# Where the tensor engine's operands start in SBUF: tiles moved to multiples of 512 bytes

## The chip, the cores and the metric

The kernel runs on one core of one Trainium2 chip, as one launch. A core has a tensor engine (TensorE, PE in the profile; its weight loads are shown apart as PEld), a vector engine (VectorE, DVE), a scalar engine (ScalarE, ACT), GpSimd (POOL) and a sync engine (SyncE, SP), which here issues all the DMAs. The on-chip memory SBUF has 128 partitions; a tile takes the same bytes in each of them, and an address below is an offset within a partition. Matmul results go to another memory, PSUM. The metric is the device time of one execution in microseconds (us).

## The reference, cut to what matters

One layer of a decoder block on 256 tokens of width 2048, all float32:

```python
mod = (silu(c) @ w_mod + b_mod).reshape(B, 6, D)          # 2048 x 12288
sh1, sc1, g1, sh2, sc2, g2 = [mod[:, i, None, :] for i in range(6)]
h = rmsnorm(x, norm_mix) * (1.0 + sc1) + sh1
proj = h @ w_in                                           # 2048 x 5660, split into 14 parts
y = concatenate([gla(...), gated_deltanet(...), pool(...), forgetting_attention(...)])
x = x + g1 * (y @ w_out)                                  # 2048 x 2048
h = rmsnorm(x, norm_ffn) * (1.0 + sc2) + sh2
gate = causal_dwconv(h @ w_gate, conv_w) + conv_b         # 2048 x 5632
x = x + g2 * ((silu(gate) * (h @ w_up)) @ w_down)         # 2048 x 5632, 5632 x 2048
return rmsnorm(x, norm_final)
```

All six parts of `mod` come from one product of `silu(c)`, a row of 2048 numbers, with `w_mod`.

## The kernel before, in words

**Large products.** All five large products with x (`w_in`, `w_out`, `w_gate`, `w_up`, `w_down`) go through the tensor engine in the dtype float32r (f32r), one pass each, and are split in two terms: an operand is rounded to f32r (the high part) and the rest is rounded again (the low part); of the four products three are taken, high by high, high by low and low by high. The helper `split` (lines 114 to 116) does this: ScalarE copies with rounding (L115), VectorE subtracts (L116, the operation at L100). `load_split` loads a weight tile of 128 partitions by 1024 numbers into `wr` (five buffers) and splits it into `wh` and `wl` (three buffers each). The activations stand split in `bigA` (tile names `HL`, `Y2`, `H2`: for each of the 16 blocks of 128 features, 256 high and 256 low numbers) and, for the down projection, in `AH` and `AL`. All matmuls are issued by the helper `mm` (L97). The stationary operand (`lhsT`) is always 128 by 128 or narrower; the moving one has 256 or 512 columns.

**Stages.** First x, the rows of `c`, biases and norms are loaded and transposed (lines 285 to 330). Then the input projection: in four groups of four feature blocks, `mods` builds the modulated activations from `w_mod` on VectorE, `gdn` accumulates the gated DeltaNet's 12 feature blocks into the six PSUM tiles `acc`, and `pair` the other columns into `ext`. The four mixers follow, with the remaining columns of the input projection put between their steps, and with the products of `c` for the other parts of `mod` (`gemv`) running beside them on the tensor engine and VectorE. Then the output projection (`project`, PSUM tiles `ext` and `wot`), the second norm, gate and up projections (`proj`, PSUM tiles `fpt`), in 11 chunks of 512 columns, and the down projection, in column chunks of 512, 512, 512, 256 and 256, with the last two `gemv` beside it.

In `proj` the moving operand is `bigA`: for a feature block, 4 matmuls with `wh` as stationary operand and 512 columns (high and low at once), and 4 with `wl` and 256 columns. In the output and down projections the moving operand is `wh` or `wl`, 512 or 256 columns wide, and the stationary one `bigA` or `AH`/`AL`.

The mixers' own matmuls (PSUM tiles `gdt`, `oxt`) and the transposes are plain float32, on other tiles.

**Order of the work.** The program is written in the order of the code with some pieces interleaved by generators; a framework places the waits. DMAs are all issued by SyncE in program order.

**Where tiles lie.** A pool places its tiles one behind the other, in the order in which their tags first appear, each at a multiple of 32 bytes; a later pool begins behind the earlier ones that are open. The pool `keep` (L90) is the first: `ident`, `crow`, `ones`, `sel`, `V1`, `V2`, `V3`, `CB`, `cond`, `mhalf`, `s2`, `sh2`, then `bigA` (32768 bytes a partition), `bigC` (16384), `ga` (4096) and `x1s`. Behind it comes `wp` with `wr`, `wh`, `wl` and `wm`, 4096 bytes each, and behind that the pools of the phases: `cp` and, inside it, `sp` for the first phase, later `ap` with `AH` and `AL`, 45056 bytes each. `crow` (16 partitions by 128 numbers, 512 bytes) holds the rows of `c` until one transpose reads them (L309). `sh2` holds 16 numbers a partition, the second norm's shift; `x1s` holds the sums of squares of the chunks of the output projection, 2 by 5 numbers, and is read once by a reduction (L1000).

Of the kernel before, what the change touches and what calls it, by code (L numbers as in the profile page):

```python
# [8 lines left out]
F32 = mybir.dt.float32  # L9
# [7 lines left out]
P = 128  # L17
D = 2048
KT = D // P
T = 256  # L20
NT = T // P
# [52 lines left out]
def trunk_kernel(ctx: ExitStack, tc: tile.TileContext, x, c, w_mod, b_mod, norm_mix, norm_ffn, w_in,  # L74
# [3 lines left out]
    nc = tc.nc  # L78
# [11 lines left out]
    keep = ctx.enter_context(tc.tile_pool(name="keep", bufs=1))  # L90
    wp = ctx.enter_context(tc.tile_pool(name="wp", bufs=3))

    def kt_(shape, name, dt=F32):
        return keep.tile(shape, dt, name=name, tag=name)
# [26 lines left out]

    ident = kt_([P, P], "ident")
    nc.sync.dma_start(ident, cst[:, K_ID:K_ID + P])
    crow = kt_([KT, P], "crow")
    nc.sync.dma_start(crow, c[0].rearrange("(k p) -> k p", p=P))
    ones = kt_([P, P], "ones")
    V.memset(ones, 1.0)

# [10 lines left out]
    mhalf = kt_([P, 16], "mhalf")  # L139
    V.memset(mhalf, -0.5)  # L140
    s2 = kt_([P, KT], "s2")
    sh2 = kt_([P, KT], "sh2")

    bigA = lambda: keep.tile([P, KT, 2 * T], F32R, name="bigA", tag="bigA")
    bigC = lambda: keep.tile([P, KT * T], F32, name="bigC", tag="bigC")
# [82 lines left out]
    with ExitStack() as ph:  # L228
# [59 lines left out]
        with ExitStack() as st:  # L288
            sp = st.enter_context(tc.tile_pool(name="sp", bufs=1, reuse_waits="tile"))
            acp = st.enter_context(tc.tile_pool(name="acp", bufs=1, space=PSUM, reuse_waits="tile"))  # L290
            xt = sp.tile([P, NT, D], F32, name="xt")
            r1 = sp.tile([P, P], F32, name="r1")
            r2 = sp.tile([54, P], F32, name="r2")
            r3 = sp.tile([2 * NF, P], F32, name="r3")
# [652 lines left out]
        chunks = ((0, 512), (512, 512), (1024, 512), (1536, 256), (1792, 256))  # L947
# [26 lines left out]
        x1 = bigC().rearrange("p (t d) -> p t d", t=NT)  # L974
        for t in range(NT):
            nc.sync.dma_start(x1[:, t], x_v[:, t])
        x1s = kt_([P, NT, len(chunks)], "x1s")
        with tc.tile_pool(name="op", bufs=2, reuse_waits="tile") as op:
            for n, (c0, w) in enumerate(chunks):
                ns, gs = slice(c0, c0 + w), slice(c0 % 1024, c0 % 1024 + w)  # L980
# [11 lines left out]
    with ExitStack() as ph:  # L992
# [69 lines left out]
        with tc.tile_pool(name="op2", bufs=1, reuse_waits="tile") as op:  # L1062
            chunks = ((0, 512), (512, 512), (1024, 512), (1536, 256), (1792, 256))
            fs = op.tile([P, NT, len(chunks)], F32, name="fs")
            f1 = op.tile([P, 4], F32, name="f1")
            for n, (c0, w) in enumerate(chunks):
# [5 lines left out]
                for g in range(NF // nk):  # L1072
                    wh, wl = load_split(wd_v, nk * g, nk, c0, w)
                    for kk in range(nk):
                        k = nk * g + kk
# [55 lines left out]
```

## Time and profile before

| | |
|---|---|
| median of three runs | 1299.27 us (1299.02 to 1306.44) |
| profiled execution, its own time | 1303.01 us |
| span of its trace | 1301.2 us |
| mean granted TensorE clock | 0.985 |
| TensorE busy | 1248.5 us, 96% of the span |
| VectorE busy | 891.0 us, 68% |
| ScalarE busy | 636.7 us, 49% |
| read from HBM | 308.51 MB, 239 GB/s over the span |

The numbers of the trace are those of one execution. Busy times of matmuls overlap, since each is counted from its start to the end of its results; the distance from one start to the next is what a stream of them costs. In a group or a timeline row stand the line, the engine, the operation, the tile written and the tiles read (the moving one first for matmuls), the shape of the weights, the shape of the moving operand, and how many. The dtype f32r is shown as f32 there. A row of a stretch gives from:to, its length, busy time and count of PE, PEld, DVE, ACT and POOL, the granted clock, the DMA engines' share and GB/s.

### The profile page before, as it was taken

To read this page: it belongs to the slowest core of one execution; us is meant where nothing else is said; L and a number is where in the kernel's file an instruction comes from. 1 tells how busy PE (TensorE), PEld (TensorE's weight loads), DVE (VectorE), ACT (ScalarE), POOL (GpSimd) and SP (SyncE) were. 2 spreads that over 40 slices of the span, in tenths; PEclk is the share of its full clock that TensorE was granted. 3 is DMA by queue.
4 is the path that set the end of the run, shared out by engine and by line. 5 is a ranking of instruction groups with operands and counts; after the bars stand their busy time and mean duration, and the time that the engine had idled before them with its cause. 6 is when DMAs were issued, how large, how long until landed. Compare 5 with 4: busy or idle time off the path is not lost.

```text
span 1301.2 us, 20372 instructions
## 1 busy us (share of the span) xinstructions
PE 1248.5 (96%) x7927; PEld 1091.0 (84%) x7927; DVE 891.0 (68%) x1201; ACT 636.7 (49%) x1000; POOL 22.7 (2%) x31
## 2 busy tenths in 40 slices
PE   2799999999999999999999999999999999999996
PEld 1799999898876788888888888888888888888896
DVE  7689797989763397676656656665656597964543
ACT  3455344774354454564545555554555454443432
POOL 0200000010000100000000000000000000000000
PEclk9799999999999999999999999999999999999998
DMA  9999998796566988556576666666665699875652
GB/s 321 277 367 378 337 341 290 259 339 212 164 236 240 318 317 276 156 165 192 163 214 190 186 187 193 190 172 206 187 187 163 219 374 359 323 243 194 192 181 81
DMA packets 174231, 311.94 MB, mean 240 GB/s; under 512 B 16172, under 2 KB 65331, under 8 KB 173495
## 3 DMA queue, kind: packets, MB, share of 16 engines
q1 hardware_dynamic: 174135, 310.65, 72.9%
q8 instruction: 62, 1.02, 0.3%
q14 instruction: 34, 0.28, 0.1%
HBM read 308.51 MB, written 2.10 MB: 239 GB/s over the span
## 4 chain that ended last, share of the span: by engine, by line
PE 92%; DMA 4%; SPq 1%; DVE 1%; ACT 1%; issue 1%; POOLq 0%; ACTq 0%; DVEq 0%
PE fpt L97 57%; PE ext L97 16%; PE wot L97 5%; PE gdt L97 4%; PE acc L97 4%; PE bgt L97 3%; DMA wm<-in_w_mod_dram 3%; PE oxt L97 2%; DMA wr<-in_w_in_dram 1%; DVE ga L103 1%; DMA ct<-in_cst_dram 0%; ACT xT L1011 0%; DVE wl L100 0%; SPq L399 0%; SPq L155 0%
## 5 line engine op out<-in xcount | busy, mean ns | idle before, releaser
L100 DVE TENSOR_TENSOR wl<-wr,wh 128x1024 fp32r<-128x1024 f32 x384 | 469.2, 1223 | 293.6 <-ACT wh L115 292.6
L115 ACT CAST wh<-wr 128x1024 fp32r<-128x1024 f32 x384 | 403.4, 1051 | 494.9 <-PE fpt L97 310.8
L97 PE MATMUL fpt<-bigA,wh 128*128 128x512 f32 x1408 | 399.6, 395 | 2.1 <-DVE bigA L103 2.1
L97 PEld LDWEIGHTS fpt<-bigA,wh 128*128 128x128 f32 x1408 | 239.3, 189 | 32.8 <-issue 2.2
L97 PEld LDWEIGHTS fpt<-bigA,wl 128*128 128x128 f32 x1408 | 222.4, 188 | 34.4 <-DVE wl L100 3.6
L97 PE MATMUL fpt<-bigA,wl 128*128 128x256 f32 x1408 | 240.4, 279 | 0.0
L103 DVE SCALAR_TENSOR_TENSOR ga<-wm,cond,ga 128x1024 f32<-128x1024 f32 x139 | 177.8, 1279 | 9.5 <-DMA wm<-in_w_mod_dram 8.6
L97 PE MATMUL fpt<-wl,AH 128*128 128x512 f32 (+1 forms) x440 | 152.9, 348 | 0.0
L97 PE MATMUL fpt<-wh,AL 128*128 128x512 f32 (+1 forms) x440 | 152.5, 347 | 0.0
L97 PE MATMUL fpt<-wh,AH 128*128 128x512 f32 (+1 forms) x440 | 142.5, 348 | 0.0
L97 PE MATMUL ext<-bigA,wh 128*128 128x256 f32 x768 | 137.0, 280 | 0.0
L97 PEld LDWEIGHTS ext<-bigA,wh 128*128 128x128 f32 x768 | 117.3, 188 | 3.1 <-DVE dS L100 0.8
L97 PE MATMUL ext<-bigA,wl 128*128 128x256 f32 x384 | 107.2, 280 | 1.7 <-DVE wl L100 1.7
L97 PEld LDWEIGHTS fpt<-wh,AH 128*128 128x128 f32 x440 | 83.3, 189 | 10.7 <-issue 0.2
L97 PEld LDWEIGHTS fpt<-wh,AL 128*128 128x128 f32 x440 | 83.3, 189 | 10.5 <-issue 0.2
L97 PEld LDWEIGHTS fpt<-wl,AH 128*128 128x128 f32 x440 | 83.3, 189 | 10.5 <-issue 0.2
L97 PE MATMUL acc<-bigA,wh 128*128 128x256 f32 x384 | 70.3, 289 | 4.7 <-ACT bigA L115 2.9
L97 PEld LDWEIGHTS ext<-bigA,wl 128*128 128x128 f32 x384 | 72.1, 188 | 3.0 <-DVE wl L100 2.1
L97 PE MATMUL ext<-wh,bigA 128*128 128x256 f32 (+1 forms) x320 | 68.0, 304 | 0.0
L97 PEld LDWEIGHTS acc<-bigA,wh 128*128 128x128 f32 x384 | 60.7, 198 | 5.1 <-ACT bigA L115 3.0
L97 PE MATMUL wot<-wh,bigA 128*128 128x512 f32 (+1 forms) x256 | 63.2, 337 | 0.0
L97 PEld LDWEIGHTS ext<-wh,bigA 128*128 128x128 f32 x320 | 51.7, 188 | 5.5 <-ACT wh L115 1.7
(340 smaller groups left out, 1191.9 us busy)
## 6 DMA issues: line engine op xcount, KB each, us to landing
wm<-in_w_mod_dram SPq DMA_DIRECT2D x192, 512.0 KB, 5.8
wr<-in_w_in_dram SPq DMA_DIRECT2D x88, 512.0 KB, 9.7
wr<-in_ffn_w_gate_dram SPq DMA_DIRECT2D x88, 512.0 KB, 3.9
wr<-in_ffn_w_up_dram SPq DMA_DIRECT2D x88, 512.0 KB, 4.4
wr<-in_ffn_w_down_dram SPq DMA_DIRECT2D x88, 512.0 KB, 4.5
wr<-in_w_out_dram SPq DMA_DIRECT2D x32, 512.0 KB, 4.2
xt<-in_x_dram SPq DMA_DIRECT2D x2, 1024.0 KB, 7.2
bigC<-in_x_dram SPq DMA_DIRECT2D x2, 1024.0 KB, 8.6
```

The costliest lines, as they stand in the source:

```text
L97: PE.matmul(o, lhsT=l, rhs=r, start=start, stop=stop, skip_group_check=True)
L100: V.tensor_tensor(out=o, in0=a, in1=b, op=op)
L103: V.scalar_tensor_tensor(out=o, in0=a, scalar=s, in1=b, op0=op0, op1=op1)
L115: S_.copy(hi, src)
```

## The change

Three tiles change their place or the room they take; no computation and no instruction is added or taken out.

- `crow` leaves the pool `keep` and becomes a tile of `sp`, the pool of the first phase, behind `xt`. Its DMA is written there, ahead of the loads of x.
- `sh2` gets room for 56 numbers instead of 16. It is used as before.
- `x1s` gets 64 numbers in each of its two rows instead of 5, of which 5 are used.

```diff
-    crow = kt_([KT, P], "crow")
-    nc.sync.dma_start(crow, c[0].rearrange("(k p) -> k p", p=P))
...
     s2 = kt_([P, KT], "s2")
-    sh2 = kt_([P, KT], "sh2")
+
+    sh2 = keep.tile([P, KT], F32, name="sh2", tag="sh2", padded_shape=[P, KT + 40])
...
             xt = sp.tile([P, NT, D], F32, name="xt")
+            crow = sp.tile([KT, P], F32, name="crow")
+            nc.sync.dma_start(crow, c[0].rearrange("(k p) -> k p", p=P))
...
-        x1s = kt_([P, NT, len(chunks)], "x1s")
+        x1s = keep.tile([P, NT, len(chunks)], F32, name="x1s", tag="x1s", padded_shape=[P, NT, 64])
```

## The prediction, made before the result was known

> **What bounds the kernel now.** I read the page first: busy times, then the chain of waits.
>
> ```profile
> span 1301.2 us, 20372 instructions
> PE 1248.5 (96%) x7927; PEld 1091.0 (84%) x7927; DVE 891.0 (68%) x1201; ACT 636.7 (49%) x1000; POOL 22.7 (2%) x31
> PE 92%; DMA 4%; SPq 1%; DVE 1%; ACT 1%; issue 1%; POOLq 0%; ACTq 0%; DVEq 0%
> ```
>
> The matmuls carry 92% of the chain that ended last. What one matmul costs in a stream therefore decides, but only where nothing else is full. The table of stretches tells where that is; its columns are the stretch, the busy time and count of each engine, the granted clock, the share of the 16 DMA engines and GB/s.
>
> ```profile
> 76.00:224.00 148.00, 146.12 (x1262) 145.21 (x1263) 127.98 (x137) 68.63 (x87) 1.46 (x3) 1.00 1.01 344
> 224.00:247.00 23.00, 23.00 (x200) 21.68 (x197) 20.09 (x51) 17.86 (x34) 0.00 (x0) 1.00 0.65 198
> 247.00:450.00 203.00, 202.44 (x1532) 162.35 (x1525) 136.61 (x241) 102.53 (x233) 7.75 (x5) 0.99 0.75 255
> 450.00:545.00 95.00, 95.00 (x522) 81.58 (x521) 72.99 (x83) 46.78 (x72) 3.75 (x3) 1.00 0.80 272
> 549.00:1015.00 466.00, 465.75 (x2660) 404.13 (x2661) 297.12 (x435) 249.12 (x381) 0.00 (x0) 1.00 0.62 185
> 1055.00:1085.00 30.00, 30.00 (x134) 24.84 (x133) 28.83 (x29) 12.92 (x15) 0.00 (x0) 1.00 1.04 397
> 1230.00:1290.00 60.00, 58.53 (x488) 58.33 (x487) 27.84 (x31) 20.80 (x26) 0.00 (x0) 1.00 0.41 126
> ```
>
> From 549 on (gate and up projections to 1015, then the down projection) TensorE is busy throughout at full clock. Before 224, and in part of the down projection (the row of 1055), the DMA engines are full as well, and VectorE nearly is (28.83 of 30 us), so a shorter matmul buys little there. From 0 to 75 the DMAs set the pace.
>
> A matmul's busy time overlaps its neighbours', so I look for the spacing of starts. The timeline gives it (start us, busy us, operation); the stretches are gate and up with the widths in blocks of four, then alternating; down at 512 and at 256 columns; input projection in two stretches; and a plain fp32 matmul, whose single record takes 379 ns.
>
> ```profile
> 665.19 1.09 PE L97 MATMUL fpt<-bigA,wh 128*128 128x512 f32 x4
> 666.12 0.62 PE L97 MATMUL fpt<-bigA,wl 128*128 128x256 f32 x4
> 666.58 0.62 PE L97 MATMUL fpt<-bigA,wh 128*128 128x512 f32 x2
> ...
> 644.79 0.40 PE L97 MATMUL fpt<-bigA,wh 128*128 128x512 f32 x1
> 645.03 0.28 PE L97 MATMUL fpt<-bigA,wl 128*128 128x256 f32 x1
> ...
> 646.21 0.40 PE L97 MATMUL fpt<-bigA,wh 128*128 128x512 f32 x1
> ...
> 1140.06 0.39 PE L97 MATMUL fpt<-wh,AL 128*128 128x512 f32 x1
> 1140.97 0.39 PE L97 MATMUL fpt<-wh,AH 128*128 128x512 f32 x1
> ...
> 1249.73 0.28 PE L97 MATMUL fpt<-wh,AL 128*128 128x256 f32 x1
> 1250.69 0.28 PE L97 MATMUL fpt<-wl,AH 128*128 128x256 f32 x1
> ...
> 120.18 0.39 PE L97 MATMUL acc<-bigA,wh 128*128 128x256 f32 x2
> 120.86 0.28 PE L97 MATMUL acc<-bigA,wl 128*128 128x256 f32 x1
> ...
> 174.88 0.40 PE L97 MATMUL acc<-bigA,wh 128*128 128x256 f32 x2
> 175.59 0.63 PE L97 MATMUL acc<-bigA,wh 128*128 128x256 f32 x4
> ...
> 490.86 0.39 PE L97 MATMUL wot<-wl,bigA 128*128 128x512 f32 x1
> 492.01 0.39 PE L97 MATMUL wot<-wl,bigA 128*128 128x512 f32 x1
> ...
> 384.14 1.03 PE L97 MATMUL oxt<-dl,pw 128*128 128x256 f32 x4
> L97 PE MATMUL oxt<-dl,pw x8: 379/379/483, 384.1 to 389.3; 128*128 128x256 f32 x8
> ```
>
> Worked out: gate/up at 512 columns (666.12 - 665.19)/4 = 232 ns, at 256 columns (666.58 - 666.12)/4 = 115; alternating, four pairs in 1.42 us, 355 a pair, some 235 and 120. Down at 512: four starts in 0.91 us, 227 ns; at 256: eight in 0.96 us, 120 ns. Input projection, 256: six in 0.68 us, 113 ns, and six in 0.71 us, 118 ns. Output projection, 512: five in 1.15 us, 230 ns. The fp32 one: (1.03 - 0.379)/3 = 217 ns for 256 columns. An fp32 matmul is run as two records and an f32r one as one; I estimate that a column of an f32r matmul takes half as long as one of an fp32 record, which gives a floor of 108 ns for 256 columns and 216 for 512. Every f32r stream lies above it: by 5 to 12 ns at 256, by 11 to 19 at 512. That excess is the only thing which a shift of addresses can get at.
>
> **The change, part by part.** All tiles keep their sizes, dtypes and instructions; only places move. I add up the tiles of the first pool in the order of the code, each rounded up to 32 bytes a partition. Before, from `ident` to `sh2`, that is 3296 bytes ahead of `bigA`; after, without `crow` and with `sh2` at 224 bytes, 2944. If `bigA` now lies at a multiple of 512, the pool starts 128 past one, and `bigA` lay at 352 past one before, `wr`, `wh`, `wl`, `wm` (behind `x1s`, 64 bytes) at 416, and so did `AH` and `AL`. Both 352 and 416 are 32 past a multiple of 64: today each f32r operand starts in the middle of a 64-byte piece, afterwards at its head. `x1s` at 512 bytes keeps the pools behind it aligned. The f32r matmuls read nothing but these tiles, save for the weights of `small` and 8 matmuls of `fox`.
>
> The excess is about 1/20 of the columns at both widths: 5 of 108, 11 of 216. A f32r stream reads 4 bytes a column at twice the pace of the fp32 one, so a read path that just keeps up at an aligned start and must fetch a piece too many otherwise would show this excess in f32r and none in fp32. I take this as likely, not as shown: no f32r operand of before starts at another offset, so the trace bounds the effect only from the two sides below.
>
> Counts come from the groups (shapes kept apart):
>
> ```profile
> L97 PE MATMUL fpt<-bigA,wh 128*128 128x512 f32 x1408 | 399.6, 395 | 2.1 <-DVE bigA L103 2.1
> L97 PE MATMUL fpt<-bigA,wl 128*128 128x256 f32 x1408 | 240.4, 279 | 0.0
> L97 PE MATMUL ext<-bigA,wh 128*128 128x256 f32 x768 | 137.0, 280 | 0.0
> L97 PE MATMUL fpt<-wl,AH 128*128 128x512 f32 x264 | 103.1, 391 | 0.0
> L97 PE MATMUL fpt<-wl,AH 128*128 128x256 f32 x176 | 49.8, 283 | 0.0
> L97 PE MATMUL wot<-wh,bigA 128*128 128x512 f32 x128 | 40.5, 396 | 0.0
> ```
>
> The down groups stand three times each (AH by `wh`, AH by `wl`, AL by `wh`): 792 wide, 528 narrow. Output projection by the loop: 288 wide, 192 narrow. Lower side, only the excess common to all streams goes (11 ns wide, 5 narrow): gate/up 1408 x 16 = 22.5 us, down 792 x 11 + 528 x 5 = 11.4, output projection 4.1, the 200 of the stretch at 224 1.0. In the mixers (247 to 450) some 650 input-projection matmuls are left (1536 of `ext` by the loops, less the 1462 matmuls between 76 and 247 that are not the 576 of `acc`); about half stand on the chain, 1.6. Before 224: 0, the DMA share is 1.01. Sum 40.6, less 1.5 (an estimate: in two stretches of some 44 us of the down projection, like the one at 1055, a third of a gain of 5% is cut by DMA): 39. Upper side, all excess goes: gate/up has a mean spacing of 465.75/2660 = 175.1 against (216 + 108)/2 = 162, 13.1 x 2816 = 36.9; down 792 x 11 + 528 x 12 = 15.0; output projection 288 x 14 + 192 x 10 = 6.0; the stretch at 224 200 x 7 = 1.4; mixers 650 x 8/2 = 2.6; sum 61.9, less 1.5: 60. Which of the streams' further excess (113 against 118 in one and the same loop) hangs on addresses I can't tell, and take half of it: 39 + 10.5 = 49.5 us.
>
> The Trainium skill (TensorE: Matmul & The Clock Gate, Wait — 56ns, not 53.3ns?) gives back-to-back starts N/2.4 + 2.5 ns at full clock, an estimated 109 and 216 ns for these widths. The fp32 row fits it and the f32r rows don't; by it the sum would be that of the upper side.
>
> The rest costs nothing. The copy of the conditioning rows stays the second on SyncE's queue, since no DMA of the program stands between its old line and its new one; its transpose ran at 3 us, and what later lies in its place in the phase's pool begins 240 us after:
>
> ```profile
> L125 SPq DMA_DIRECT2D crow<-in_c_dram x1: 419/419/419, 1.2 to 1.2; - x1
> L309 PE MATMUL ext<-ident,crow x1: 252/252/252, 3.0 to 3.0; 16*128 16x16 f32 x1
> L1000 DVE TENSOR_REDUCE s<-x1s x1: 164/164/164, 544.8 to 544.8; 128x2 f32<-128x10 f32 x1
> ```
>
> Were it moved behind the loads of x, two issues of 0.42 us would go ahead of it, 0.8 us. The one reduction of `x1s` now steps over 64 elements between rows instead of 5: between 0 and a second 164 ns. DMAs land at other offsets; the row at 1055 already runs at 397 GB/s, so I give them 0, from -2 to +2 us.
>
> Profiled execution: 1303.0 us (1301.2 of span), 3.7 above the median of 1299.3. 1303.0 - 49.5 = 1253.5, on the scale of the median 1250.
>
> **Rivals.** *No effect: the pace is f32r's own.* For it: the excess grows with the width, 227 being twice 113.5, as a rate would, where one lost fetch per instruction would cost both widths alike. Against: the same array and operands lose nothing in fp32. Time: 1299, and the same if the layout isn't what I added up. The Trainium skill (SBUF — State Buffer, Specifications (TRN2)) speaks for this rival: it counts SBUF in lines of 16 bytes, and an offset of 32 is a line's head already; its section on operand start alignment says that it timed nothing. No row of before can decide it.
>
> *Slower: the stationary and the moving operand collide.* Afterwards both start at the same place modulo 512 in every f32r matmul. Today that holds in the down projection alone (416 both), and there 256 columns take 120 ns, the slowest of all streams of that width; against it, its 512-wide ones, at 227, are the fastest. If the collision spreads and takes the dearest spacings everywhere while nothing is won: gate/up from 175.1 to half of 355 gives 2.4 x 2816 = 6.8 us, down wide from 227 to 235 gives 6.3, output projection 288 x 5 = 1.4, input projection 1462 x (120 - 115.7) = 6.3 (115.7 is 169.1 us over 1462), mixers 650 x 4.3/2 = 1.4: 22 us, 1321. It decides from somewhat over half of that, 13 us, on.
>
> *Gained but hidden.* DMA or VectorE take over after 549. The stretch at 549 has DMA at 0.62 and VectorE busy 297 of 466 us, so only the down projection can lose; with all of its 11 us lost 1261. That lies within the forecast.
>
> **How the numbers follow.** Forecast with its bounds, 1238 to 1262: 0.58, which takes in a partial gain. No effect: 0.32. Slower: 0.10. About 1% is what a measurement of this kernel can tell from no change, so faster has 0.58, within 1% 0.32, slower 0.10. Both of the first two cases must be in the range: 1238 (60 us won) to 1304 (no effect, with 5 us of scatter), which leaves out the slower case and a little below.
>
> **What would show it.** Right: the mean of one `fpt<-bigA,wh` at 512 columns falls from 395 ns by 11 to 16, of `fpt<-bigA,wl` at 256 from 279 by 5 to 8, the starts at 1140 stand 216 ns apart, and the stretch from gate to the end of the down projection shortens by 34 to 50 us while the head up to 224 stays. The weight loads' 188 ns needn't change. No effect: 227 and 113 stay the smallest spacings. Collision: 120 ns turns up in the input projection. The forecast is wrong if the spacings fall and the span doesn't, since I hold that after 549 nothing else is near its limit for long.

## The result, and the profile after

The changed kernel takes 1312.9 us (median of 5, 1310.4 to 1313.1), the kernel before, beside it, 1300.6 (1299.0 to 1306.4). The means are 1312.2 and 1301.6; the ratio is 1.0081, 95% interval 1.0055 to 1.0107: slower by 0.8%, or 10.5 us. The profiled execution of after took 1310.4 us, 1308.6 of them span, against 1303.0 and 1301.2 before.

The page of after, the same lines as before (length, busy times, the chain's shares by engine):

```profile
span 1308.6 us, 20372 instructions
PE 1258.6 (96%) x7927; PEld 1101.5 (84%) x7927; DVE 890.6 (68%) x1201; ACT 637.6 (49%) x1000; POOL 23.0 (2%) x31
PE 92%; DMA 4%; DVE 1%; SPq 1%; ACT 1%; issue 1%; POOLq 0%; ACTq 0%; DVEq 0%
```

The same instructions, and TensorE's busy time is 10.1 us longer and that of its weight loads 10.5; the other engines stay. The table of stretches (columns as before) shows where:

```profile
76.00:224.00 148.00, 146.32 (x1225) 145.70 (x1224) 123.60 (x132) 67.59 (x86) 0.00 (x0) 1.00 0.95 333
549.00:1015.00 466.00, 463.86 (x2622) 402.29 (x2623) 293.94 (x433) 248.58 (x383) 0.00 (x0) 1.00 0.61 182
1055.00:1085.00 30.00, 30.00 (x134) 24.69 (x133) 28.58 (x33) 13.86 (x17) 0.00 (x0) 1.00 1.03 407
```

In the input projection 1225 matmuls fit where 1262 did, in gate and up 2622 in place of 2660, in the down projection 134 as before. The granted clock is 1.00 in all three, and the DMA share isn't higher. The groups of matmuls with their mean duration, shapes kept apart:

```profile
L97 PE MATMUL fpt<-bigA,wh 128*128 128x512 f32 x1408 | 400.0, 396 | 2.1 <-DVE bigA L103 2.1
L97 PE MATMUL fpt<-bigA,wl 128*128 128x256 f32 x1408 | 244.9, 282 | 0.0
L97 PE MATMUL ext<-bigA,wh 128*128 128x256 f32 x768 | 142.1, 285 | 0.0
L97 PE MATMUL fpt<-wl,AH 128*128 128x512 f32 x264 | 103.2, 391 | 0.0
L97 PE MATMUL fpt<-wl,AH 128*128 128x256 f32 x176 | 49.8, 283 | 0.0
L97 PE MATMUL wot<-wh,bigA 128*128 128x512 f32 x128 | 40.1, 392 | 0.0
```

The 512-wide ones stay (396 for 395) or, in the output projection, get shorter (392 for 396); those with 256 columns and `bigA` get longer (282 for 279, 285 for 280); the down projection stays to the nanosecond. The timeline of after, in three streams (gate, input, down):

```profile
661.93 1.09 PE L97 MATMUL fpt<-bigA,wh 128*128 128x512 f32 x4
662.86 0.63 PE L97 MATMUL fpt<-bigA,wl 128*128 128x256 f32 x4
663.33 1.09 PE L97 MATMUL fpt<-bigA,wh 128*128 128x512 f32 x4
...
120.75 0.40 PE L97 MATMUL acc<-bigA,wh 128*128 128x256 f32 x2
...
124.71 0.52 PE L97 MATMUL acc<-bigA,wh 128*128 128x256 f32 x3
...
1145.81 0.39 PE L97 MATMUL fpt<-wh,AL 128*128 128x512 f32 x1
...
1148.08 0.39 PE L97 MATMUL fpt<-wh,AH 128*128 128x512 f32 x1
```

Gate: 0.93/4 = 232 ns wide as before, 0.47/4 = 118 narrow in place of 115. Input: 33 starts lie between 120.75 and 124.71, 120.0 ns each; before there stood 113 and 118. Down, ten starts in 2.27 us: 227, as before. Over all starts of the two traces, the mean pair of gate and up takes 234.2 + 119.4 = 353.6 ns in place of 233.8 + 116.1 = 349.9, and 3.7 x 1408 is 5.2 us.

The extent of the groups closes the account. The rows give shortest, median and longest duration in ns, then first and last start; the first two are of before, the last two of after:

```profile
L97 PE MATMUL fpt<-bigA,wh x1408: 388/397/766, 549.3 to 1041.2; 128*128 128x512 f32 x176
L97 PE MATMUL fpt<-wh,AH x440: 278/389/793, 1041.9 to 1288.0; 128*128 128x512 f32 x88, 128*128 128x256 f32 x59
```
```profile
L97 PE MATMUL fpt<-bigA,wh x1408: 387/396/628, 551.8 to 1048.9; 128*128 128x512 f32 x176
L97 PE MATMUL fpt<-wh,AH x440: 277/389/798, 1049.7 to 1295.8; 128*128 128x512 f32 x88, 128*128 128x256 f32 x59
```

Gate and up begin 2.5 us later (551.8 for 549.3) and last 5.3 longer (497.9 for 492.6), the down projection takes 246.1 both times, and what follows is 0.4 shorter: 7.4 us in all, the difference of the two spans. Ahead of gate and up one execution scatters by some us; the experiments below give a better figure for that part.

### The profile page after: what moved, and what is told of

It is laid out like the page before. It is cut to its first block, busy times and chain, and to the rows that moved or that the text cites. A ratio compares the mean times of both kernels' runs of the same rounds, so it can differ in the third digit from the quotient of the medians.

```text
span 1308.6 us, 20372 instructions
## 1 busy us (share of the span) xinstructions
PE 1258.6 (96%) x7927; PEld 1101.5 (84%) x7927; DVE 890.6 (68%) x1201; ACT 637.6 (49%) x1000; POOL 23.0 (2%) x31
## 4 chain that ended last, share of the span: by engine, by line
PE 92%; DMA 4%; DVE 1%; SPq 1%; ACT 1%; issue 1%; POOLq 0%; ACTq 0%; DVEq 0%
PE fpt L97 57%; PE ext L97 16%; PE wot L97 5%; PE acc L97 4%; PE gdt L97 4%; PE bgt L97 3%; PE oxt L97 2%; DMA wr<-in_w_in_dram 2%; DMA wm<-in_w_mod_dram 1%; DVE ga L103 1%; DMA ct<-in_cst_dram 0%; ACT xT L1012 0%; SPq L154 0%; SPq L361 0%; DVE wl L100 0%
## 5 line engine op out<-in xcount | busy, mean ns | idle before, releaser
L97 PE MATMUL fpt<-bigA,wl 128*128 128x256 f32 x1408 | 244.9, 282 | 0.0
L103 DVE SCALAR_TENSOR_TENSOR ga<-wm,cond,ga 128x1024 f32<-128x1024 f32 x139 | 177.9, 1280 | 10.1 <-DMA wm<-in_w_mod_dram 9.1
L97 PE MATMUL ext<-bigA,wh 128*128 128x256 f32 x768 | 142.1, 285 | 0.0
L97 PEld LDWEIGHTS ext<-bigA,wh 128*128 128x128 f32 x768 | 120.1, 192 | 3.1 <-issue 1.2
L97 PEld LDWEIGHTS fpt<-wh,AL 128*128 128x128 f32 x440 | 83.3, 189 | 10.5 <-issue 0.2
```

The costliest lines, as they stand in the source:

```text
L97: PE.matmul(o, lhsT=l, rhs=r, start=start, stop=stop, skip_group_check=True)
L103: V.scalar_tensor_tensor(out=o, in0=a, scalar=s, in1=b, op0=op0, op1=op1)
```

## The experiments

**The theories.** The addresses of the built kernels are as the prediction added them up: before, `bigA` 352, and `wh`, `wl`, `AH`, `AL` 416 past a multiple of 512; after, `bigA`, `wh` and `wl` at 0. So two things changed at once. *A:* the place of each operand counts (the prediction's reason, now with the opposite sign). *R:* the distance of the two operands of a matmul counts, taken modulo some power of two. It was 64 wherever `bigA` takes part, and is 0 now; between `AH` and `wh` it was 0 and is 0. In the layer the distance is the weights' address less that of `bigA`, in the streams below that of the stationary operand less that of the moving one; the two differ in the output projection alone, where `bigA` is the stationary operand, so that 64 is 192 there.

In a steady stream a single duration tells the spacing, being 163 ns longer: 276 goes with 113, 281 with 118, 283 with 120, 389 with 227, 396 with 233. Spacings given without a row are means over all starts of the group in the trace.

**Streams alone, distance in steps of 32 bytes.** A kernel that leaves the whole layer out and runs only streams of f32r matmuls on one tile:

```diff
+for c in range(16):                       # narrow_a .. narrow_p, wide_a .. wide_p
...
+    for i in range(32):
+        mm(o[i % 4], FAR + 32 * c + 512 * (i % 4), 0, n)       # stationary, moving, columns
...
+for c in range(0, 16, 2):                 # half_a .. half_o
...
+        mm(o[i % 4], FAR + 32 + 32 * c + 512 * (i % 4), 32, 256)
```

> This kernel leaves the whole layer out and streams f32r matmuls alone; its time says nothing, its spacings do. Each group writes a PSUM tile of its own name: narrow_a to narrow_p and wide_a to wide_p (256 and 512 columns, one fixed moving operand at a multiple of 512 bytes, four stationary operands 512 bytes apart that start 32 bytes further for each letter, so a is 0, c is 64, i is 256, p is 480 bytes past a multiple of 512 from the moving one), half_a, half_c, ... half_o (256 columns, both operands 32 bytes further than in narrow) and gate_a to gate_p (the order of the gate projection, four wide then four narrow). The mean duration of one in the trace is its spacing plus some 163 ns: 276 stands for 113, 281 for 118, 283 for 120. Theory R, the distance of the two operands modulo 512 bytes decides: narrow_a and half_a both at 283, narrow_c and half_c both at 276 to 281, and a curve over the letters that is the same in narrow and half. Theory A, the place of an operand on its own decides: every letter of narrow at one duration, 283, and every letter of half at another, 276 to 281. If neither decides (neighbouring traffic does): one duration for all.

The extents of some streams; letter a is distance 0, c 64, i 256, and in `half` both operands lie 32 bytes further:

```profile
L83 PE MATMUL narrow_a<-B x32: 278/283/283, 46.6 to 50.3; 128*128 128x256 f32 x32
L83 PE MATMUL narrow_c<-B x32: 281/281/283, 54.2 to 57.9; 128*128 128x256 f32 x32
L83 PE MATMUL narrow_i<-B x32: 278/283/283, 77.0 to 80.7; 128*128 128x256 f32 x32
L83 PE MATMUL wide_a<-B x32: 387/389/398, 107.4 to 114.4; 128*128 128x512 f32 x32
L83 PE MATMUL wide_c<-B x32: 393/396/398, 122.1 to 129.4; 128*128 128x512 f32 x32
L83 PE MATMUL half_a<-B x32: 278/283/283, 226.1 to 229.8; 128*128 128x256 f32 x32
```

At 256 columns distance 0 is the slow one (119.7 ns, 117.8 at 64); at 512 it is the fast one (228.1, 233.4 at 64). Shifting both operands by 32 changes little (119.4 at distance 0; at 128, the largest difference, 118.7 for 120.1). Distance 256 is like 0: the period is 256 bytes, not 512 as expected. The gate's streams of this kernel were put in another order than meant and are taken up again below. What is seen is R, and it is what the kernel before showed all along: its down projection, at distance 0, ran at 120 and 227, its other streams, at 64 or 192, at 113 to 118 and 229 to 235.

**The layer, one thing at a time.** Four layouts of the kernel before:

```diff
+# distance 0, bigA left at 352
+x1s = keep.tile([P, NT, len(chunks)], F32, name="x1s", tag="x1s", padded_shape=[P, NT, 64])
+# distance 256: padded_shape=[P, NT, 32];  distance 192: padded_shape=[P, NT, 24]
+# aligned, distance 64: crow and sh2 as in the change, x1s as before
+sh2 = keep.tile([P, KT], F32, name="sh2", tag="sh2", padded_shape=[P, KT + 40])
```

> The kernel before with x1s at 512 bytes instead of 64 and nothing else: bigA stays 352 bytes past a multiple of 512, wr, wh, wl, wm, AH and AL move from 416 to 352, so that the distance of the two operands becomes 0 modulo 512 as in the changed kernel, at places that are multiples of 32 only. Theory R (distance): as the changed kernel, 1310 to 1313 us, 256-column matmuls of the input projection at 283 to 285 ns. Theory A (place): as the kernel before, 1299 to 1303 us, 279 to 280 ns.

> The changed kernel with x1s at 64 bytes as before: bigA at a multiple of 512, crow in the first phase's pool, but wr, wh, wl, wm, AH and AL 64 bytes past a multiple, the distance of the kernel before. Theory R: as the kernel before, 1299 to 1303 us. Theory A (a multiple of 512 costs): between the two, about 1306, since one operand of each matmul is still at one. If the move of crow were what costs: as the changed kernel, 1312.

> The kernel before with x1s at 256 bytes: the distance between bigA and the weight tiles is 256 modulo 512 instead of 64. Theory R: another time than both kernels, by some us either way, with all 256-column matmuls of the input projection and of gate and up at another spacing than 113 to 120; the down projection, whose tiles move together, stays at 120 and 227. Theory A: as the kernel before, 1299 to 1303 us.

> The kernel before with x1s at 192 bytes instead of 64: distance 192 between bigA and the weight tiles, 64 seen from the output projection's side. Theory R: by the streams measured alone, wide ones 229 at 192 against 233 at 64 bytes, narrow ones 118 at both, where the kernel before also has many at 113: gate and up win 1408 x 4 = 5.6 us on the wide and lose up to 1408 x 2 = 2.8 on the narrow, the input projection loses up to 3, so 1297 to 1303. Theory A: as before, 1299 to 1303, with unchanged spacings.

The 256-wide matmuls of gate and up and, for 192, of the output projection; one fence each for distance 0, aligned at 64, 256 and 192:

```profile
L97 PE MATMUL fpt<-bigA,wl 128*128 128x256 f32 x1408 | 244.1, 281 | 0.0
```
```profile
L97 PE MATMUL fpt<-bigA,wl 128*128 128x256 f32 x1408 | 240.3, 279 | 0.0
```
```profile
L97 PE MATMUL fpt<-bigA,wl 128*128 128x256 f32 x1408 | 244.2, 281 | 0.0
```
```profile
L97 PE MATMUL fpt<-bigA,wh 128*128 128x512 f32 x1408 | 396.0, 393 | 2.1 <-DVE bigA L103 2.1
L97 PE MATMUL wot<-wh,bigA 128*128 128x512 f32 x128 | 41.0, 399 | 0.0
L97 PE MATMUL wot<-wh,bigA 128*128 128x256 f32 x128 | 21.9, 276 | 0.0
```

| layout | us | ratio to before, 95% interval | gate and up, ns wide + narrow |
|---|---|---|---|
| distance 0, `bigA` at 352 | 1312.3 | 1.0087 (1.0068 to 1.0107) | 233.4 + 118.9 |
| aligned, distance 64 | 1301.8 | 0.9998 (0.9981 to 1.0014) | 233.8 + 116.1 |
| distance 256 | 1312.4 | 1.0088 (1.0067 to 1.0109) | 233.5 + 118.9 |
| distance 192 | 1303.2 | 0.9994 (0.9982 to 1.0006) | 231.3 + 116.8 |

Each ratio is to the kernel before on the same chip, which took 1301.2 us beside the first three and 1303.7 beside the fourth. Distance 0 without any alignment gives the whole slowdown, alignment without distance 0 gives none of it and no gain, and 256, expected to differ from both kernels, is as bad as 0. A is out as the cause of the slowdown, and the move of `crow` and of `sh2` is seen to cost nothing. At 192 gate and up win 1.8 ns a pair, and the 512-wide output projection loses 4 ns each, since its own distance goes from 192 to 64; the total does not change clear of noise. The output projection of before, of distance 192 and of after (its own distance 192, 64 and 0) ran its 512-wide matmuls at 229.0, 233.3 and 227.0 ns; the streams alone gave 228.8, 233.4 and 228.1 at these distances.

The four layouts also size the part ahead of gate and up. Its first matmul starts at 551.8, 555.0 and 553.2 us in the three profiles at distance 0 (after, and the two here), mean 553.3; in that of before and in the six profiles of the other layouts of this section between 545.8 and 550.0, mean 548.3. So 5.0 us come from there, and gate and up last 496.7 us in the mean of the three against 492.6: 9.1 us together, of the 10.5; where the rest lies isn't shown.

**The down projection moved to 64.** A gap of 64 bytes ahead of `AH` and `AL`:

```diff
+gap = wp.tile([P, 16], F32, name="gap", tag="gap", bufs=1)
+V.memset(gap, 0.0)
 ap_ = ph.enter_context(tc.tile_pool(name="ap", bufs=1, reuse_waits="tile"))
```

> The kernel before with 64 bytes between wm and AH, so that only the distance between wh, wl and AH, AL changes, from 0 to 64 bytes. Theory R: only the down projection changes: its 528 matmuls of 256 columns go from 120 ns to 113 to 118 (-1 to -3.7 us), its 792 of 512 columns from 227 to between 227 and 233 (0 to +5 us); all other streams keep their spacings; 1298 to 1305 us. Theory A: nothing changes anywhere.

The groups of the down projection in that kernel:

```profile
L97 PE MATMUL fpt<-wl,AH 128*128 128x512 f32 x264 | 104.7, 397 | 0.0
L97 PE MATMUL fpt<-wl,AH 128*128 128x256 f32 x176 | 48.5, 276 | 0.0
```

Both flip: narrow from 283 to 276 (120.0 to 113.3 ns), wide from 391 to 397 (226.8 to 233.3). By these means 792 x 6.5 - 528 x 6.7 = +1.6 us, and the down projection's 246.1 us become 247.7. The ratio is 1.0007 (0.9992 to 1.0021). The effect thus sits in the pair of operands, not in `bigA` or in the stage.

**Is 113 f32r's own pace?** A second kernel of streams, among them a stationary operand of 32 columns with the moving one at eight places (0, 4, 16, 32, 48, 64, 128, 256 bytes), and plain fp32:

```diff
+PE.matmul(o[i % 4][0:32, 0:256], lhsT=at(FAR + 1024, 32), rhs=at(place, 256), start=True, stop=True, ...)
```

> Again only streams, the layer is left out. gatewide_/gatenarrow_ a to p: the gate projection's own order (four matmuls of 512 columns, four of 256, the moving operand moving on by 2048 bytes), the letters again 32 bytes of distance each. in_ a to p: the input projection's order, 256 columns, the same stationary operand twice and then its low part. thin_a to thin_h: a stationary operand of 32 columns, the moving one 0, 4, 16, 32, 48, 64, 128, 256 bytes past a multiple of 512. plain_a, plain_c: float32, distances 0 and 64. Theory R now with a period of 256 bytes: i to p repeat a to h; gate at a shows what the changed kernel showed (234 and 119 ns of spacing), at c what the kernel before showed (232 to 234 and 115 to 116); in_a 120, in_c 113 to 118. The prediction's step (an f32r operand that starts off a multiple of 64 is fetched one piece too many): thin_a, thin_f, thin_g, thin_h at 107 to 109 and the others at 113. The rival that the pace is f32r's own: 113 for all of thin. If the stationary read is what collides, thin never shows 118 or 120. plain: 216 to 217 at both.

Places 0, 4 and 16, and plain fp32 at distance 0 (16 matmuls in the code, 32 records):

```profile
L113 PE MATMUL thin_a<-B x24: 280/280/281, 272.2 to 274.9; 128*32 128x256 f32 x24
L113 PE MATMUL thin_b<-B x24: 281/283/283, 275.0 to 277.7; 128*32 128x256 f32 x24
L113 PE MATMUL thin_c<-B x24: 275/275/282, 277.9 to 280.5; 128*32 128x256 f32 x24
...
L120 PE MATMUL plain_a<-xt x32: 377/379/379, 294.3 to 301.0; 128*128 128x256 f32 x32
```

The eight give 117.8, 119.9, 113.9, 117.3, 113.8, 113.4, 113.7 and 114.0 ns. None comes near 108, at any place, though only a quarter of the stationary operand is read. So 113 is the best pace that f32r shows here; what sets it isn't shown. Two expectations failed: 113 for all eight, and that so narrow a stationary operand never shows 118 or 120. A record of plain fp32 takes 215.8 ns for 256 columns at distances 0 and 64 alike, and a matmul has two: 432 ns, nearly four times that of f32r. In the orders of the gate and the input projection the distances from 256 on repeat those below it. But places 0 and 256 have the same distance modulo 256 and differ by 3.8 ns: the distance isn't all.

**Steps of 8 bytes.** The same with 32 distances from 0 to 248, in the orders of three projections:

```diff
+for c in range(32):                       # ..._a to ..._z, ..._A to ..._F
...
+    last[0] = mm(t[f], w + 8 * c + 2048 * (j % 2) + 512 * f, 2048 * j, n)
```

> Streams of f32r matmuls alone, the layer is left out. The distance of stationary and moving operand is raised from 0 in steps of 8 bytes (letters a to z, then A to F; 32 distances, 0 to 248), in the order of the gate projection (four of 512 columns, four of 256), of the input projection (256), and of the down projection at 512 and at 256. Theory R (the distance modulo 256 alone sets the spacing): the distances that are multiples of 32 (a, e, i, m, q, u, y, C) repeat the earlier streams in the order of the gate projection: 231, 231, 232, 234, 233, 233, 231, 233 ns at 512 columns and 118, 119, 115, 119, 117, 120, 116, 117 at 256, and the input order 120, 118, 118, 117, 118, 120, 118, 118, within 1 ns; those between lie within the same bounds (113 to 120, 227 to 235) and no distance gives 227 and 113 at once in the gate order. Rival (what collides is found at a finer step than 32 bytes): some distances between have both widths at 227 and 113, and a layout at such a distance would save some 1408 x 4 + 1408 x 3 ns, 10 us, in gate and up. Either way nothing below 113 or 226: below that the first theory of the prediction (an excess over 108 and 216 that an address can take away) would live again.

Input order at 0, 64 and 88 bytes, then the 512-wide down order at 120:

```profile
L83 PE MATMUL in_a<-B x48: 278/283/283, 315.8 to 321.5; 128*128 128x256 f32 x48
L83 PE MATMUL in_i<-B x48: 276/276/287, 361.3 to 366.7; 128*128 128x256 f32 x48
L83 PE MATMUL in_l<-B x48: 276/276/282, 378.2 to 383.5; 128*128 128x256 f32 x48
...
L83 PE MATMUL downwide_p<-B x24: 389/389/396, 580.8 to 586.0; 128*128 128x512 f32 x24
```

Nothing lies below 113.5 or 226.8. No distance has both widths at their best: in the gate's order the pairs reach from 345.8 ns (192 bytes) to 353.4 (160), with 347.6 at 64. Two expectations failed. Distance 24 gave 121.6 ns in the input order, above the bound of 120, so 0 is not the slowest. And the input order at 64 gave 113.7 ns here and 117.8 in the earlier kernel of streams: the same distance has two levels, as the prediction's rows showed at 120 and at 175 us of the kernel before.

**What collides?** Streams whose two operands change places in turn, and the gate's widths with a distance each:

```diff
+for c, (n, s0, s1, m0, m1) in enumerate(((256, 0, 0, 0, 0), (256, 64, 64, 0, 0), (256, 0, 64, 0, 64), (256, 64, 0, 0, 64), ...
...
+    w, m = (s1, m1) if j % 2 else (s0, m0)
+    last[0] = mm(o[j % 4], FAR + w + 512 * (j % 8), m + 2048 * (j // 4 % 6), n)
...
```

> Streams of f32r matmuls alone, the layer is left out. First, twelve streams in which stationary and moving operand change their places from one matmul to the next (256 columns: swap_a to swap_f, 512: swap_g to swap_l). Theory O (what counts is the distance of the two operands of the same matmul): swap_a and swap_c (own distance 0) about 120 ns, swap_b and swap_d (64) 113 to 115; wide, swap_g and swap_i 227, swap_h and swap_j about 233. Theory N (while one matmul streams, the stationary operand of the next is read; that distance counts): swap_d (own 64, next 0) is like swap_a, 120, and swap_c (own 0, next 64 or 192) is not, 113 to 118; wide, swap_j like swap_g, 227, and swap_i like swap_h. swap_e, swap_f, swap_k and swap_l (half of the pairs at 0) lie between. Then the gate projection's two widths with a distance of their own each, in blocks of four and in turn. In blocks, both theories: 512 columns at 0 and 256 at 64 (block c) give 227 to 231 and 113 to 115, some 5 to 8 ns a pair less than today's 64 and 64 (block b). In turn, theory O: turn c is the fastest, N: turn d (0 and 64 exchanged). If either pair comes to 342 ns or less against some 350 of 64 and 64, the gate and up projections (1408 pairs) have up to 11 us to win by moving one of the two tiles of weights.

Four of the 512-wide streams, then the gate's wide ones in turn with the narrow ones, all at 0 (a) and all at 64 (b):

```profile
L83 PE MATMUL swap_g<-B x48: 388/389/397, 82.3 to 93.0; 128*128 128x512 f32 x48
L83 PE MATMUL swap_h<-B x48: 392/396/398, 93.2 to 104.2; 128*128 128x512 f32 x48
L83 PE MATMUL swap_i<-B x48: 388/394/398, 104.4 to 115.3; 128*128 128x512 f32 x48
L83 PE MATMUL swap_j<-B x48: 388/393/397, 115.5 to 126.4; 128*128 128x512 f32 x48
...
L83 PE MATMUL turnwide_a<-B x24: 391/391/396, 282.6 to 290.6; 128*128 128x512 f32 x24
L83 PE MATMUL turnwide_b<-B x24: 392/397/398, 290.9 to 299.0; 128*128 128x512 f32 x24
```

Neither theory holds. Fixed distances give 227.3 (0) and 233.4 (64); with own distance 0 and the next one's off it 231.9, with own 64 or 192 and the next one's 0 231.4. Narrow: 119.8, 117.8, 117.2 and 120.0. Own and next distance both count. Blocks with 0 for the wide and 64 for the narrow ones took 349.9 ns a pair, more than 64 and 64 (347.2). The least of all pairs was 345.0 (240 and 192 in blocks, not tried in the layer) and none came to 342: the hoped-for 11 us aren't to be had in this way. The order counts as well: in blocks of four, 0 for both widths took 349.8 ns and 64 for both 347.2; in turn, 346.9 and 353.1. So 0 loses in the one order and wins in the other; in the layer blocks prevail (461 of the 1408 wide matmuls of gate and up are followed by a narrow one before, 352 if all stood in blocks of four). What in the read of two operands makes the pattern stays open.

**A layout that uses it.** 192 in gate and up only, the rest as before; and, as its control, the same shift of all tiles by 128 bytes without the other distance:

```diff
-    bigA = lambda: keep.tile([P, KT, 2 * T], F32R, name="bigA", tag="bigA")
+    bigA = lambda o=32: keep.tile([P, KT * 2 * T + 32], F32R, name="bigA", tag="bigA")[:, o:o + KT * 2 * T].rearrange("p (k n) -> p k n", k=KT)
...
-        H2 = bigA()
+        H2 = bigA(0)
...
# the control, instead:
-    sh2 = kt_([P, KT], "sh2")
+    sh2 = keep.tile([P, KT], F32, name="sh2", tag="sh2", padded_shape=[P, KT + 32])
```

> The kernel before, with one change: the tile of bigA is 128 bytes longer, and the gate and up projections' activations (H2) start at its head, those of the input and output projections (HL, Y2) 128 bytes behind it. So the distance of stationary and moving operand stays 64 in the input projection and 192 (stationary less moving) in the output projection and 0 in the down projection, as before, and becomes 192 in gate and up, where a layout with 192 throughout has shown 231.3 and 116.8 ns against 233.8 and 116.1. The theory that the distance modulo 256 sets the spacing expects of gate and up 1408 x 1.8 ns = 2.5 us, all else unchanged: ratio 0.998, some 1299 us against 1301.5. If the spacing hung on the place of the tiles rather than on the distance, or on what ran before, nothing would have to change in gate and up, or the other stages would change with it: ratio 1.000 or above.

> The kernel before with one change: sh2 takes 128 bytes more, so that every tile behind it lies 128 bytes further on. All distances of stationary and moving operand are those of before; the places are those of the version with two distances, but for H2, which lies 128 bytes behind its place there. If the distance alone decides: ratio 1.000, spacings as before (233.8 and 116.1 in gate and up, acc 117, the 256-wide wot 118). If the place of the tiles, at an equal distance, has its share: acc 113 and wot 113 as in the version with two distances, and some of its 0.2% gain here too, with gate and up unchanged.

> The version with two distances once more, on the same chip as the shift by 128 bytes, from which it differs in the distance of gate and up alone (192 in place of 64). Distance alone: ratio to before 0.998 again, and 0.998 to the shifted kernel, with 231 to 232 and 117 ns in gate and up against 234 and 116. If the gain came from the place of the tiles: both kernels the same.

Gate and up with the down projection, then a 256-wide group of the output projection, each first of the layout (on the chip that it shared with the control) and then of the control; the last row is of the kernel before:

```profile
L97 PE MATMUL fpt<-bigA,wh x1408: 388/392/764, 548.3 to 1038.9; 128*128 128x512 f32 x176
L97 PE MATMUL fpt<-wh,AH x440: 278/389/803, 1039.6 to 1285.6; 128*128 128x512 f32 x88, 128*128 128x256 f32 x59
```
```profile
L97 PE MATMUL fpt<-bigA,wh x1408: 388/397/765, 547.6 to 1039.3; 128*128 128x512 f32 x176
L97 PE MATMUL fpt<-wh,AH x440: 278/389/803, 1040.0 to 1286.2; 128*128 128x512 f32 x88, 128*128 128x256 f32 x59
```
```profile
L97 PE MATMUL wot<-wh,bigA 128*128 128x256 f32 x128 | 21.9, 276 | 0.0
```
```profile
L97 PE MATMUL wot<-wh,bigA 128*128 128x256 f32 x128 | 21.9, 276 | 0.0
```
```profile
L97 PE MATMUL wot<-wh,bigA 128*128 128x256 f32 x128 | 22.8, 279 | 0.0
```

The layout takes 1300.4 us, ratio to before 0.9981 (0.9968 to 0.9994), and the second time 1300.7, 0.9987 (0.9974 to 0.9999); the control 1301.7, 1.0000 (0.9988 to 1.0012). So there is a layout a little faster than both kernels, by 0.1 to 0.2%. Gate and up take 491.3 us against 492.4 in the control (231.9 + 117.0 and 233.6 + 116.1 ns), 1.1 us of the 2.5 expected. The extent alone would not prove even that: the kernel with its down projection at 64, whose gate and up kept the distance of before, took 491.0, with fewer waits in between. Counting only starts within 300 ns of each other, the layout has 230.4 + 117.0 ns, the control and the kernel before 232.2 + 116.1, and the one with the down projection at 64 232.2 + 115.9: 0.7 to 0.9 ns a pair, 1.0 to 1.3 us. The control shows something else: at an unchanged distance its 256-wide output projection runs at 113 ns, where before and the aligned layout had 118. So the distance isn't the only thing that counts; whether the place or what ran before chooses the level can't be told from this. By the spacings it is worth 192 x 4.5 ns = 0.9 us, less than the control's interval can tell.

## Why the prediction was wrong

**The step that failed** is the cost given to the alignment: that an f32r stream whose operands start "in the middle of a 64-byte piece" must fetch "a piece too many" and would be faster without it. Under it lay the floor: that a column of f32r takes half as long as one of an fp32 record, 108 and 216 ns. With the operands aligned and the distance kept, 233.8 + 116.1 ns stayed to the decimal. And there was no such excess to win: at all places tried, with 128 and with 32 stationary columns, no stream went below 113 and 226. All terms of the sum (22.5, 11.4, 4.1, 1.0 and 1.6 us on the lower side) were differences against a floor that no f32r stream here reached. The floor was half of what the fp32 record took, so that fp32 loses nothing against it was no evidence of its own. The rule quoted from the Trainium skill (TensorE: Matmul & The Clock Gate, Wait — 56ns, not 53.3ns?), 109 and 216 ns by the estimate for 256 and 512 columns, holds for no f32r stream here, and the fp32 row doesn't fit it as the prediction says: its record of 256 columns took 217 ns there and 215.8 alone, what the rule gives for 512.

**"No effect"** had the pace right, with 227 being twice 113.5 as its reason. It lacked that the change sets a distance as well as a place.

**"Slower"** had the mechanism: both operands at the same place, 120 ns spreading from the down projection to the input projection, as it named for its sign. Its 22 us were twice too much, the measured being 10.5. Gate and up came close (6.8 foreseen; 3.4 to 5.3 in the three profiles at distance 0, 4.1 in the mean). The down projection's 6.3 did not come, since its distance was 0 already and stayed 0, and the output projection's 512-wide ones became faster (229.0 to 227.0 ns), since distance 0 favours that width; input projection, mixers and output projection together cost 5.0 in place of 9.1. The price rested on "takes the dearest spacings everywhere", though the same rows showed both widths at distance 0 side by side: 120 and 227. Read as one pair of numbers, they said that narrow streams would lose some 4 ns and wide ones nothing; interleaved in gate and up, the wide ones indeed kept theirs (233.8 to 234.2), winning nothing either. The chance of 0.10 was the other mistake, and the range ended at 1304 because of it. By its own count, which lets the slower case begin 13 us on, the 10.5 us even fall to "within 1%", 0.32, though the mechanism is that of "slower".

The Trainium skill (SBUF — State Buffer, A bandwidth-pool intuition that's wrong (but worth ruling out)) gives TensorE a second independent read port for the weight loads. If independent is taken to cover addresses, of which the page says nothing there, the place of the one operand against the other shouldn't matter. The layout with `bigA` unmoved and distance 0 went from 116.1 to 118.9 ns and 0.87% slower in all: the measurement decides.

**What held.** The addresses were right, and so was that the move of `crow`, the wider `sh2` and the stepping reduction cost nothing that can be seen. Nothing else than TensorE is near its limit after 549: in gate and up the starts within 300 ns of each other went from 348.3 to 352.1 ns a pair, and 1408 x 3.8 ns = 5.4 us came out as 5.3 us more of time.

## What to carry to other kernels

Alignment by itself bought nothing for f32r; the distance between the stationary and the moving operand, modulo 256 bytes, was worth 0.8% of this kernel, which is nearly all matmuls. In streams of one width, 64 and 88 bytes were among the best for 256 columns and 0 among the best for 512; no layout tried suited both, and the order of the widths can turn the choice round. So measure the spacing in the order that the kernel has. Before a floor is used in a sum, look for a stream that reaches it, and where one stage already has the layout that a change brings to all, read both of its widths as the forecast.

## What the runs showed of the hardware

- f32r ran at 113 ns per 256 columns and 227 per 512 at best, plain fp32 at two records of 215.8 ns per 256 columns; over all distances tried the spacing of f32r in streams alone varied by 8 ns at either width (113.5 to 121.7 and 226.7 to 234.3), that of fp32, at 0 and 64, not at all.
- The pattern has a period of 256 bytes: 0 and 256 alike, in streams alone and in the layer (1.0087 and 1.0088). With 32 stationary columns 0 and 256 differed (117.8 and 114.0 ns).
- In streams of one width, 0 is among the slowest distances at 256 columns (120 ns) and among the fastest at 512 (227). With both widths in one stream the order decides: 0 against 64 cost 2.6 ns a pair in blocks of four and won 6.2 in turn.
- Equal distances can settle on two levels (113 or 118 ns at 64 bytes). A shift of all tiles by 128 bytes changed the level in the output projection; what else chooses it is open.
